# ConvFFN pairs of a decoder step: two weight sums and two low parts moved from VectorE to transfers that add

## The chip, the cores and the metric

The kernel runs on one core of one Trainium2 chip. The metric is the device time of one execution in microseconds; the median of three runs is given. The core has TensorE (PE; its weight loads are shown as PEld), VectorE (DVE), ScalarE (ACT), GpSimd (POOL) and SyncE (SP), and 16 DMA engines that all queues share.

## The reference

One layer of a hybrid decoder is computed for 512 prompt tokens and 8 x 8 sample tokens, 576 in all: a normalized input projection, a short convolution branch and a windowed attention branch, their merge, and then a ConvFFN. The change is in the ConvFFN, which is, cut to what matters:

```python
h2 = _rmsnorm(x, norm2_g) * (1.0 + sc2) + sh2
a, val = jnp.split(h2 @ w_up, 2, axis=-1)          # 1024 x 2 * 2816
ac, new_ffn = _causal_conv(a, ffn_buf, ffn_conv_w)   # width 3, along the tokens
x = x + g2 * ((jax.nn.gelu(ac, approximate=False) * val) @ w_down)
```

## The kernel before

All operands are float32. A product keeps that precision by a split: `hi` is the operand rounded to TensorE's fp32r (a copy by ScalarE), `lo` is source minus `hi` (a subtraction by VectorE), and a product is three matmuls, hi x hi, hi x lo and lo x hi. Weights are stationary tiles of 128 x 128; the tokens are the moving side.

The 2816 hidden columns are 22 tiles of 128, in groups 0 to 7, 8 to 15 and 16 to 21. After the hidden tiles of a group, the down-projection of that group adds to the residual: eight products, one for each 128 output columns. Tiles 0 to 3 are computed plainly. Tiles 4 to 21 are **pairs** (`FfnPair`): the gate tile and the value tile of the same number are computed together, as a product of 2 x 2 blocks by Winograd's scheme with seven block products instead of eight. The blocks are gate and value, the two halves of the inner dimension (4 slices of 128 each), and the two halves of the tokens (288 each).

Per pair, the weights are loaded as two tiles of 128 x 1024 (512 KB), `ra` for the value and `rb` for the gate, into the pool `raw` with four buffers. A DMA row is 512 B. With c0 and c1 for the first and second four slices, VectorE makes four sums of 128 x 512:

- `sums1` (lines 305 to 308): `s3 = ra.c0 + rb.c0`, and `rb.c0 += rb.c1`;
- `sums2` (lines 310 to 312): `ra.c0 += rb.c0`, and `ra.c1 += ra.c0`.

Four groups of weights are split in high and low parts: A is `ra` before its sums, B is `rb` after `sums1`, C is `ra` after `sums2`, D is `s3`. A, B and C are 128 x 1024 and go to pools `whi` and `wlo` with five buffers each; D is 128 x 512 and goes to slots of a common pool of 57. `pair_weights` gives these as steps with names: `ah` is the high part of A, `al` its low part, and so for `bh`, `bl`, `ch`, `cl`, `dh`, `dl`.

`pair_product` (lines 334 to 377) is the seven parts of 12 matmuls each; after part n it calls `steps[n]`. Part 1 uses A, part 2 C, part 3 B, part 4 A, part 5 B, part 6 D, part 7 C. The results of parts 1 and 3 are copied from their bank by ScalarE (`p`); VectorE forms the differences `uv`; and the gate and value are combined by VectorE, the last 64 tokens by POOL (lines 1536 and 1548).

While pair m runs, `beside_pair` (lines 1561 to 1571) prepares the weights of pair m+1 and does the rest of pair m-1 (convolution taps, gelu, product, split), and the loads of pair m+2 are issued. During a down-projection `in_turn` (lines 329 to 332) does the steps of the next group's first pair after the products 4 to 7. Ahead of pair 4 the steps are written out by hand between the products of tiles 2 and 3 (lines 1660 to 1683).

From the FFN on, TensorE, VectorE and ScalarE keep the program's order (`pinned`). The order on POOL and SyncE is set by a scheduler with a simulated timeline. Each engine and each queue works in the order that results. SyncE issues the loads; a load waits until its buffer is free. Lines 104 to 112 are a helper that issues the operations, so most instructions carry line 109; SyncE's weight loads carry line 148.

Of the kernel before, what the change touches and what calls it, by code (L numbers as in the profile page):

```python
# [10 lines left out]
F32 = mybir.dt.float32  # L11
F32R = mybir.dt.float32r
AF = mybir.ActivationFunctionType
ALU = mybir.AluOpType
AX = mybir.AxisListType

P = 128
D = 1024
NK = D // P
# [6 lines left out]
FF = 2816  # L26
# [9 lines left out]
S_BUFS = 5  # L36
# [33 lines left out]
def step_kernel(ctx: ExitStack, tc: tile.TileContext, ins: dict, outs: list):  # L70
    nc = tc.nc
# [5 lines left out]
    wp = ctx.enter_context(tc.tile_pool(name="wp", bufs=3))  # L77
# [8 lines left out]
    def nm(s):  # L86
        cnt[0] += 1
        return f"{s}{cnt[0]}"

    def slot(s, dt=F32, shape=None):  # L90
        return ap_.tile(shape or [P, NT], dt, tag="a", name=nm(s))
# [22 lines left out]
    pe, act, dve, pool = (InOrder(e) for e in (nc.tensor, nc.scalar, nc.vector, nc.gpsimd))  # L114
# [30 lines left out]
    def load_w(src, nk):  # L145

        raw = wp.tile([P, nk, P], F32, tag="raw", name=nm("raw"), bufs=W_BUFS)
        nc.sync.dma_start(raw, src)
        return raw
# [56 lines left out]
    def product(w, xs):  # L206
        ps = mmps()
        for k in range(len(xs)):
            kstep(halves(ps), w, xs, k)
            tick()  # L210
        return pf(ps)
# [17 lines left out]
    class PairOperands:  # L229
# [38 lines left out]
        def low(self):  # L268
            for lo, src, hi in ((self.tl, self.t, self.th), (self.nl, self.r[0][:, :HT], self.nh)):
                dve.tensor_tensor(out=lo, in0=src, in1=hi.bitcast(F32), op=ALU.subtract)  # L270
# [12 lines left out]
    def pair_weights(ra, rb):  # L283

        c0, c1 = slice(0, 4), slice(4, 8)
        w = {}

        def add(out, x, y):
            dve.tensor_tensor(out=out, in0=x, in1=y, op=ALU.add)

        def tiles():
            return [wp.tile([P, NK, P], F32R, tag=t, name=nm(t), bufs=S_BUFS) for t in ("whi", "wlo")]

        def high(name, src, get):
            w[name] = hi, lo = get()
            act.activation(hi, src, AF.Copy)

        def low(name, src):
            hi, lo = w[name]
            dve.tensor_tensor(out=lo, in0=src, in1=hi.bitcast(F32), op=ALU.subtract)  # L300

        def s3_slots():
            return slot("wh", F32R, [P, 4, P]), slot("wl", F32R, [P, 4, P])

        def sums1():
            w["raw"] = slot("s3", shape=[P, 4, P])
            add(w["raw"], ra[:, c0], rb[:, c0])
            add(rb[:, c0], rb[:, c0], rb[:, c1])

        def sums2():  # L310
            add(ra[:, c0], ra[:, c0], rb[:, c0])
            add(ra[:, c1], ra[:, c1], ra[:, c0])

        def named(n0, n1, name):
            hi, lo = w[name]
            w[n0] = (lambda k: hi[:, k, :]), (lambda k: lo[:, k, :])
            if n1:
                w[n1] = (lambda k: hi[:, k + 4, :]), (lambda k: lo[:, k + 4, :])

        def one(name, src, get, n0, n1):  # L320
            return (lambda: (high(name, src(), get), named(n0, n1, name))), (lambda: low(name, src()))

        ah, al = one("A", lambda: ra, tiles, "a0", "a1")
        dh, dl = one("D", lambda: w["raw"], s3_slots, "s3", None)
        bh, bl = one("B", lambda: rb, tiles, "s1", "b1")
        ch, cl = one("C", lambda: ra, tiles, "s2", "s4")
        return w, dict(sums1=sums1, sums2=sums2, ah=ah, al=al, bh=bh, bl=bl, ch=ch, cl=cl, dh=dh, dl=dl)

    def in_turn(t):

        order = {0: "sums1 ah al", 2: "dh dl sums2", 3: "bh bl", 4: "ch cl"}
        return {at: (lambda names=names: [t[n]() for n in names.split()]) for at, names in order.items()}
# [46 lines left out]
    def kpm(w, m0, k0=0, nk=NK):  # L379
        return w[k0 * P : (k0 + nk) * P, m0 : m0 + P].rearrange("(k p) m -> p k m", p=P)  # L380
# [311 lines left out]
    for x in range(2):  # L692
        for y in range(2):
            c = slice(2 * y, 2 * y + 2)
            tc.keep_in_program_order(nc.gpsimd.dma_start(xT_dram[x, :, c], xTt[x][:, c]))
    kT = []
    for j in (2, 0, 1):
        t = slot("kT")
# [20 lines left out]
    for raw in raws:  # L719
        hi = wp.tile([P, 4, 256], F32R, tag="whi", name=nm("whi"), bufs=S_BUFS)  # L720
        lo = wp.tile([P, 4, 256], F32R, tag="wlo", name=nm("wlo"), bufs=S_BUFS)
# [14 lines left out]
    for i in range(5):  # L736
        ps = aux()
        for k in range(NK):
            whi, wlo = (x[:, k % 4, :] for x in wv[k // 4])
# [9 lines left out]
    for i in (3, 4):  # L749
# [3 lines left out]
        t = slot("kout", shape=[P, 256])  # L753
# [21 lines left out]
    def queries(t, ps=None):  # L775
# [52 lines left out]
        out=sel,  # L828
        in0=snk.rearrange("p (h g) -> p h g", h=4),
        in1=ind.unsqueeze(1).to_broadcast([P, 4, 4]),  # L830
        op=ALU.mult,
# [331 lines left out]
    for m in range(NK):  # L1163
        if m in (5, 6):
            src, dst = ((ins["cache_k_win"], nks), (ins["cache_v_win"], nvs))[m - 5]
# [15 lines left out]
        if m == 1:  # L1181
# [9 lines left out]
            out=b10(u)[:, :, 2:10], in0=b8(sv(ps)), in1=b8(sv(c_sb)), op=ALU.mult  # L1191
# [44 lines left out]
    for m in range(NK - 1):  # L1236
        w = weights(kpm(wco, m * P), NK)
# [6 lines left out]
    w, steps = pair_weights(*raws[0])  # L1244
# [55 lines left out]
    def residual(ps, xt, blk, c0=0, c1=NT):  # L1300

        p1 = min(c1, 512)
        dve.scalar_tensor_tensor(
            out=xt[:, c0:p1], in0=ps[:, : p1 - c0], scalar=modT[:, blk, 0:1], in1=xt[:, c0:p1],
            op0=ALU.mult, op1=ALU.add,
        )
        if c1 > 512:
            t = sp.tile([P, 64], F32, tag="rt", name=nm("rt"))
            dve.tensor_tensor(
                out=b8(t), in0=b8(ps[:, p1 - c0 :]), in1=bc(modT[:, blk, 1:9]), op=ALU.mult  # L1310
            )
            dve.tensor_tensor(out=sv(xt), in0=sv(xt), in1=t, op=ALU.add)
# [196 lines left out]
    class FfnPair(FfnTile):  # L1509


        def __init__(self, m):
            super().__init__(m)
            self.raws = [load_w(kpm(w_up, c + m * P), NK) for c in (FF, 0)]

        def prepare(self):
            self.w, self.steps = pair_weights(*self.raws)
            return self.steps

        def run(self, steps):  # L1520
# [40 lines left out]
    def beside_pair(p, t):  # L1561

        none = lambda: None
        f = lambda n: t[n] if t else none
        g = lambda n: getattr(p, n) if p else none
        return {
            0: [f("ah"), g("first_tap"), f("sums1"), f("al"), g("taps")],
            1: [f("dh"), f("bh"), g("gelu")],
            2: [f("dl"), f("sums2"), f("bl"), g("times")],
            4: [f("ch"), g("high"), f("cl"), g("low")],  # L1570
        }

    def down_load(m, m0, m1):
# [87 lines left out]
    nxt = FfnPair(5)  # L1661
    ops[3].sums()
    ops[3].high()
    steps["ah"]()
    a3 = product(w_a3, h2)
    value(tiles[2], v2)
    tiles[2].low()
    ops[3].low()
    steps["sums1"]()
    steps["al"]()  # L1670
    steps["dh"]()
    steps["bh"]()
    steps["dl"]()
    v3 = product(w_v3, h2)
    start(tiles[3], a3)
    steps["sums2"]()
    tiles[3].taps()
    tiles[3].gelu()
    steps["ch"]()
    steps["bl"]()  # L1680
    steps["cl"]()
    value(tiles[3], v3)
    tiles[3].low()

# [2 lines left out]
    for m0, m1 in FCH:  # L1687
# [3 lines left out]
        for m in range(max(m0, 4), m1):  # L1691
            pair = pairs.pop(m)
            beside = [{0: n3}] if m == 4 else []
            if m + 1 < m1:
                if m + 2 < m1:
                    pairs[m + 2] = FfnPair(m + 2)
                beside.append(beside_pair(before, pairs[m + 1].prepare()))
            else:
                wd = {}
                raw = [down_load(j, m0, m1) for j in range(2)]  # L1700
                beside.append(beside_pair(before, None))
                beside.append({2: [lambda: wd.update({0: split_w(raw[0])})],
                               4: [lambda: wd.update({1: split_w(raw[1])})]})
            pair.run(merged(*beside))
            before = pair
# [6 lines left out]
        if m1 < NF:  # L1712
            pairs = {m1: FfnPair(m1)}
            steps = None
            ps = [mmps() for _ in range(2)]
            n = m1 - m0
            for k0, k1 in ((0, n - 2), (n - 2, n)):
                for j in range(2):
                    for k in range(k0, k1):
                        kstep(halves(ps[j]), wd[j], fa, k)  # L1720
            wd[2] = split_w(down_load(2, m0, m1))
            for j in range(2):
                residual(pf(ps[j]), x1[j], 40 + j)
            for m in range(2, NK):
                if m + 1 < NK:
                    wd[m + 1] = split_w(down_load(m + 1, m0, m1))
                acc_m = product(wd[m], fa)
                if m == 4:
                    steps = in_turn(pairs[m1].prepare())
                    steps[0]()  # L1730
                elif m > 4:
                    steps[m - 3]()
                if m == NK - 1:
                    pairs[m1 + 1] = FfnPair(m1 + 1)
                residual(acc_m, x1[m], 40 + m)
            continue
        pinned.clear()
# [105 lines left out]
```

## Time and profile before

| what | value |
|---|---|
| median of three runs | 1001.3 us (1000.7 to 1001.51) |
| span of the profiled execution | 999.2 us; no other time is given for it |
| busy, PE / PEld / DVE / ACT / POOL | 983.2 / 942.1 / 672.2 / 449.6 / 100.4 us |
| granted TensorE clock | 0.998 |
| DMA | 119.18 MB, mean 119 GB/s |

Pair 4 starts at about 640 us, the last pair ends at about 946 us. Busy time of an engine doesn't say that it bounds: what counts is which wait ends last. A busy TensorE isn't TensorE at its peak, as the ends of matmuls are modelled. Names in the rows are those of the program without numbers, so the tile `s3` is shown as `s`, and all `raw` tiles as `raw`.

### The profile page before, as it was taken

How to read it: one execution, taken by the hardware profiler on the slowest of the kernel's cores; microseconds unless marked ns; L12 is line 12 of the kernel's file. 1: busy time of each engine (PE TensorE's matmuls, PEld its weight loads, DVE VectorE, ACT ScalarE, POOL GpSimd, SP SyncE). 2: the span in 40 equal slices, each digit the busy share in tenths (PEclk: the TensorE clock that was granted, in tenths of full speed). 3: DMA queues.
4: the chain of work that ended last, by engine and by line, in shares of the span. 5: the costliest groups of instructions: out<-in, count | busy, mean ns of one | idle time of the engine just before them, and what ended most of it. 6: DMA issues, size and time to landing. Idle time of an engine off the chain costs nothing.

```text
span 999.2 us, 18724 instructions
## 1 busy us (share of the span) xinstructions
PE 983.2 (98%) x7516; PEld 942.1 (94%) x7516; DVE 672.2 (67%) x1243; ACT 449.6 (45%) x837; POOL 100.4 (10%) x271
## 2 busy tenths in 40 slices
PE   7999999999999999999999999999999999999997
PEld 6799999999989889999889999999999999999997
DVE  5637666666563367888454568896569995579954
ACT  5354545444544225545232347554225553235453
POOL 2222111100010000000000021011001110001120
PEclk9999999999999999999999999999999999999999
DMA  9983322333423822235972302233233222323302
GB/s 305 320 247 95 107 84 78 93 110 111 141 65 88 289 97 85 86 103 156 342 230 73 107 6 79 65 85 106 85 95 95 86 85 86 106 67 100 110 9 95
DMA packets 173481, 119.18 MB, mean 119 GB/s; under 512 B 6887, under 2 KB 160846, under 8 KB 173106
## 3 DMA queue, kind: packets, MB, share of 16 engines
q1 hardware_dynamic: 169954, 107.00, 35.1%
q0 software_dynamic: 3296, 10.73, 3.4%
q8 instruction: 59, 0.97, 0.4%
q14 instruction: 28, 0.23, 0.1%
q10 hardware_dynamic: 144, 0.26, 0.1%
HBM read 109.17 MB, written 7.35 MB: 117 GB/s over the span
## 4 chain that ended last, share of the span: by engine, by line
PE 88%; DVE 5%; ACT 2%; DMA 2%; issue 2%; SPq 0%; POOL 0%; POOLq 0%; DVEq 0%; ACTq 0%
PE mm L109 64%; PE aux L109 21%; PE aux L1104 2%; PE aux L1019 1%; DMA ad<-in_w_ada 1%; DVE wlo L109 1%; DMA raw<-in_w_in 1%; ACT whi L109 1%; SPq L385 0%; DVE raw L109 0%; DVE cy L109 0%; ACT y L109 0%; DVE uv L109 0%; DVE tl L109 0%; DVE fl L109 0%
## 5 line engine op out<-in xcount | busy, mean ns | idle before, releaser
L109 ACT ACTIVATE whi<-raw 128x1024 fp32r<-128x1024 f32 (+3 forms) x166 | 168.1, 1024 | 200.8 <-PE mm L109 106.9
L109 DVE TENSOR_TENSOR wlo<-raw,whi 128x1024 fp32r<-128x1024 f32 (+3 forms) x166 | 195.3, 1183 | 48.3 <-ACT whi L109 46.2
L109 PE MATMUL mm<-hh,whi 128*128 128x256 f32 (+2 forms) x560 | 127.6, 304 | 0.5 <-ACT hh L109 0.5
L109 PE MATMUL mm<-hh,wlo 128*128 128x256 f32 (+2 forms) x560 | 122.1, 295 | 0.0
L109 PE MATMUL mm<-hl,whi 128*128 128x256 f32 (+2 forms) x560 | 121.0, 295 | 0.1
L109 PEld LDWEIGHTS mm<-hh,whi 128*128 128x128 f32 x560 | 91.6, 188 | 8.1 <-issue 6.6
L109 PEld LDWEIGHTS mm<-hl,whi 128*128 128x128 f32 x560 | 93.7, 188 | 0.7 <-DVE hl L109 0.5
L109 PEld LDWEIGHTS mm<-hh,wlo 128*128 128x128 f32 x560 | 94.2, 188 | 0.0
L109 DVE SCALAR_TENSOR_TENSOR x<-mm,modT,x 128x512 f32<-128x512 f32 (+1 forms) x33 | 22.6, 686 | 70.6 <-PE mm L109 70.5
L109 PE MATMUL mm<-fl,whi 128*128 128x256 f32 (+1 forms) x304 | 65.4, 296 | 0.0
L109 PE MATMUL mm<-fh,whi 128*128 128x256 f32 (+1 forms) x304 | 64.8, 295 | 0.3 <-DVE rt L109 0.3
L109 PE MATMUL mm<-fh,wlo 128*128 128x256 f32 (+1 forms) x304 | 64.7, 294 | 0.0
L109 PE MATMUL mm<-th,whi 128*128 128x288 f32 x208 | 61.6, 296 | 0.7 <-DVE uv L109 0.7
L109 PE MATMUL mm<-th,wlo 128*128 128x288 f32 x208 | 61.4, 295 | 0.5 <-DVE wlo L109 0.5
L109 PE MATMUL mm<-tl,whi 128*128 128x288 f32 x208 | 61.2, 294 | 0.0
L109 PEld LDWEIGHTS mm<-fh,whi 128*128 128x128 f32 x304 | 50.6, 188 | 0.5 <-PE mm L109 0.5
L109 PEld LDWEIGHTS mm<-fh,wlo 128*128 128x128 f32 x304 | 51.0, 188 | 0.0
L109 PEld LDWEIGHTS mm<-fl,whi 128*128 128x128 f32 x304 | 50.9, 188 | 0.0
L109 PE MATMUL aux<-2h,whi 128*128 128x288 f32 (+2 forms) x160 | 47.3, 295 | 0.8 <-ACT p L109 0.8
L109 PE MATMUL aux<-2h,wlo 128*128 128x288 f32 (+2 forms) x160 | 47.2, 295 | 0.0
L109 PE MATMUL aux<-2l,whi 128*128 128x288 f32 (+2 forms) x160 | 47.0, 294 | 0.0
L870 ACT ACTIVATE s<-s,nmx 128x256 f32<-128x256 f32 (+1 forms) x72 | 34.1, 475 | 25.5 <-DVE nmx L867 17.4
(310 smaller groups left out, 2569.8 us busy)
## 6 DMA issues: line engine op xcount, KB each, us to landing
raw<-in_w_in SPq DMA_DIRECT2D x52, 512.0 KB, 4.2
raw<-in_w_up SPq DMA_DIRECT2D x44, 512.0 KB, 3.8
ada<-in_w_ada SPq DMA_DIRECT2D x64, 256.0 KB, 6.0
ad<-in_w_ada SPq DMA_DIRECT2D x32, 256.0 KB, 6.3
raw<-in_w_down SPq DMA_DIRECT2D x16, 512.0 KB, 3.5
raw<-in_w_conv_out SPq DMA_DIRECT2D x8, 512.0 KB, 3.5
raw<-in_w_attn_out SPq DMA_DIRECT2D x8, 512.0 KB, 3.5
raw<-in_w_mix_out SPq DMA_DIRECT2D x8, 512.0 KB, 5.6
```

The lines of the kernel that those rows point to most:

```text
L109: done = getattr(self.engine, name)(*args, **kwargs)
L870: nc.scalar.activation(s[x // 2][:, x % 2, :w], s[x // 2][:, x % 2, :w], AF.Exp, bias=nmx[:, x : x + 1], accum_out=den[:, x : x + 1],)
L1019: done = nc.tensor.matmul(O[HALF[par], :256], vt(i - nkt + 1 + kt)[:, hd * 64 : hd * 64 + 64], pts[kt][:, par * 256 : par * 256 + 256], st ...
L1104: done = nc.tensor.matmul(ps[32 * j : 32 * j + 32, :], cT[:, k, :], cols[k][j], start=(k == 1), stop=(k == NK - 2),)
```

## The change

1. The pair allocates `s3` itself, and SyncE loads `ra.c0` a second time into it (256 KB, from the value columns). `sums1` becomes two transfers issued by POOL that read DRAM and add to what is in SBUF: the first four slices of the gate columns onto `s3`, the second four onto `rb.c0`. VectorE's two sums go.
2. The low parts of B and C: ScalarE writes the high part, then a second copy with scale -1 writes `lo = -hi`, and a transfer issued by POOL from SBUF to SBUF adds the source, so that `lo = source - hi`. VectorE's two subtractions go. A and D are split as before.
3. The steps move: beside a pair, `sums2` and B come after part 1, D after part 2, C after part 3, and the `sums1` of pair m+2 are asked for after part 4. In a down-projection, `sums1` come after product 3, A and `sums2` after product 4, B after 5, D and C after 6, and the second pair of the next group is loaded and summed after product 7. Ahead of pair 4 the order by hand is changed in the same sense.

The number of matmuls doesn't change.

```diff
+    def add_transfer(out, src):
+        return pool.dma_start(out, src, accum_op=ALU.add)
+
+    def pair_weights_moved(ra, rb, s3):
...
+        def ah():
+            w["A"] = hi, lo = tiles()
+            act.activation(hi, ra, AF.Copy)
+            named("a0", "a1", "A")
+        def low(name, src):
+            hi, lo = w[name]
+            dve.tensor_tensor(out=lo, in0=src, in1=hi.bitcast(F32), op=ALU.subtract)
+        def sums2():
+            dve.tensor_tensor(out=ra[:, c0], in0=ra[:, c0], in1=rb[:, c0], op=ALU.add)
+            dve.tensor_tensor(out=ra[:, c1], in0=ra[:, c1], in1=ra[:, c0], op=ALU.add)
...
+        def moved(name, src, n0, n1):
+            w[name] = hi, lo = tiles()
+            act.activation(hi, src, AF.Copy)
+            act.activation(lo, hi.bitcast(F32), AF.Copy, scale=-1.0)
+            named(n0, n1, name)
+            add_transfer(lo.bitcast(F32), src)
...
+    def in_turn_moved(t):
+        order = {0: "ah al sums2", 2: "b", 3: "dh dl c"}
...
 class FfnPair(FfnTile):
             self.raws = [load_w(kpm(w_up, c + m * P), NK) for c in (FF, 0)]
+            self.s3 = slot("s3", shape=[P, 4, P])
+            nc.sync.dma_start(self.s3, kpm(w_up, FF + m * P, 0, 4))
+
+        def sums1(self):
+            m = self.m
+            add_transfer(self.s3, kpm(w_up, m * P, 0, 4))
+            add_transfer(self.raws[1][:, 0:4], kpm(w_up, m * P, 4, 4))
...
 beside_pair
-            0: [f("ah"), g("first_tap"), f("sums1"), f("al"), g("taps")],
-            1: [f("dh"), f("bh"), g("gelu")],
-            2: [f("dl"), f("sums2"), f("bl"), g("times")],
-            4: [f("ch"), g("high"), f("cl"), g("low")],
+            0: [f("ah"), g("first_tap"), f("al"), g("taps")],
+            1: [f("sums2"), f("b"), g("gelu")],
+            2: [f("dh"), f("dl"), g("times")],
+            3: [f("c")],
+            4: [g("high"), g("low")],
...
 ahead of pair 4
     ops[3].high()
+    pair.sums1()
     steps["ah"]()
     a3 = product(w_a3, h2)
     value(tiles[2], v2)
     tiles[2].low()
     ops[3].low()
-    steps["sums1"]()
     steps["al"]()
+    steps["sums2"]()
+    steps["b"]()
+    v3 = product(w_v3, h2)
     steps["dh"]()
-    steps["bh"]()
     steps["dl"]()
-    v3 = product(w_v3, h2)
+    steps["c"]()
+    nxt.sums1()
     start(tiles[3], a3)
-    steps["sums2"]()
     tiles[3].taps()
     tiles[3].gelu()
-    steps["ch"]()
-    steps["bl"]()
-    steps["cl"]()
     value(tiles[3], v3)
...
 beside a pair, and in a down-projection
+                if m + 2 < m1:
+                    beside.append({4: [pairs[m + 2].sums1]})
...
-                    steps = in_turn(pairs[m1].prepare())
+                    steps = in_turn_moved(pairs[m1].prepare())
...
+                if m == 3:
+                    pairs[m1].sums1()
                 if m == NK - 1:
                     pairs[m1 + 1] = FfnPair(m1 + 1)
+                    pairs[m1 + 1].sums1()
```

More of the change, by code (lines that the diff above doesn't have):

```diff
@@ L327, in pair_weights, with tiles, named, dh @@
         return w, dict(sums1=sums1, sums2=sums2, ah=ah, al=al, bh=bh, bl=bl, ch=ch, cl=cl, dh=dh, dl=dl)
+    def add_transfer(out, src):
+        return pool.dma_start(out, src, accum_op=ALU.add)
+    def pair_weights_moved(ra, rb, s3):
+        w = {}
+        c0, c1 = slice(0, 4), slice(4, 8)
+        def tiles():
+            return [wp.tile([P, NK, P], F32R, tag=t, name=nm(t), bufs=S_BUFS) for t in ("whi", "wlo")]
+        def named(n0, n1, name):
+            hi, lo = w[name]
+            w[n0] = (lambda k: hi[:, k, :]), (lambda k: lo[:, k, :])
+            if n1:
+                w[n1] = (lambda k: hi[:, k + 4, :]), (lambda k: lo[:, k + 4, :])
+        def ah():
[3 more added lines that the diff above has]
+        def low(name, src):
+            hi, lo = w[name]
+            dve.tensor_tensor(out=lo, in0=src, in1=hi.bitcast(F32), op=ALU.subtract)
+        def sums2():
+            dve.tensor_tensor(out=ra[:, c0], in0=ra[:, c0], in1=rb[:, c0], op=ALU.add)
+            dve.tensor_tensor(out=ra[:, c1], in0=ra[:, c1], in1=ra[:, c0], op=ALU.add)
+        def dh():
+            w["D"] = hi, lo = slot("wh", F32R, [P, 4, P]), slot("wl", F32R, [P, 4, P])
+            act.activation(hi, s3, AF.Copy)
+            named("s3", None, "D")
+        def moved(name, src, n0, n1):
[4 more added lines that the diff above has]
+            add_transfer(lo.bitcast(F32), src)
+        return w, dict(
+            sums2=sums2, ah=ah, al=lambda: low("A", ra), dh=dh, dl=lambda: low("D", s3),
+            b=lambda: moved("B", rb, "s1", "b1"), c=lambda: moved("C", ra, "s2", "s4"),
+        )
+    def in_turn_moved(t):
+        order = {0: "ah al sums2", 2: "b", 3: "dh dl c"}
+        return {at: (lambda names=names: [t[n]() for n in names.split()]) for at, names in order.items()}
     def in_turn(t):
@@ L1514, in __init__ @@
             self.raws = [load_w(kpm(w_up, c + m * P), NK) for c in (FF, 0)]
+            self.s3 = slot("s3", shape=[P, 4, P])
[4 more added lines that the diff above has]
+            add_transfer(self.raws[1][:, 0:4], kpm(w_up, m * P, 4, 4))
         def prepare(self):
-            self.w, self.steps = pair_weights(*self.raws)
+            self.w, self.steps = pair_weights_moved(*self.raws, self.s3)
             return self.steps
@@ L1728, in step_kernel @@
                 if m == 4:
-                    steps = in_turn(pairs[m1].prepare())
+                    steps = in_turn_moved(pairs[m1].prepare())
                     steps[0]()
-                elif m > 4:
+                elif m > 4 and m - 3 in steps:
                     steps[m - 3]()
+                if m == 3:
+                    pairs[m1].sums1()
                 if m == NK - 1:
                     pairs[m1 + 1] = FfnPair(m1 + 1)
+                    pairs[m1 + 1].sums1()
                 residual(acc_m, x1[m], 40 + m)
```

## The prediction

> **What bounds the kernel now.** I read the page's busy times first, then the waits of TensorE from 480 us on, then the chain of waits and a table of stretches in the pair stage, and last the DMA views.
>
> ```profile
> PE 983.2 (98%) x7516; PEld 942.1 (94%) x7516; DVE 672.2 (67%) x1243; ACT 449.6 (45%) x837; POOL 100.4 (10%) x271
> ```
> ```profile
> PE aux L109 <- ACT p L109: 0.8, 1, 0.8
> PE mm L109 <- DVE uv L109: 0.7, 3, 0.3
> PE mm L109 <- DVE wlo L109: 0.5, 1, 0.5
> PE mm L109 <- DVE rt L109: 0.3, 1, 0.3
> PE mm L109 <- ACT sq L109: 0.2, 1, 0.2
> ```
> TensorE is busy for 98% of the span, and after 480 us it waits 2.5 us in all. The first three of these waits, 2.0 us, belong to the pairs that the change touches. So the change can win little; how much it can lose is the question.
>
> One part of a pair product is 12 matmuls (chain of waits), seven parts are a pair, and the stretches give a pair's period (columns: us, busy us of PE, PEld, DVE, ACT and POOL with counts, clock, DMA share, GB/s):
>
> ```profile
> 748.78 1.58 PE aux L109 x12
> ```
> ```profile
> 739.26:750.37 11.11, 11.11 (x87) 11.11 (x86) 9.37 (x15) 5.31 (x7) 0.82 (x3) 1.00 0.34 94
> 772.58:783.67 11.09, 11.09 (x87) 11.09 (x86) 10.95 (x17) 6.04 (x9) 1.40 (x5) 1.00 0.31 92
> 806.40:818.02 11.62, 11.36 (x84) 11.16 (x85) 11.48 (x19) 5.41 (x8) 1.76 (x6) 1.00 0.31 93
> ```
> Bound by TensorE, a pair takes 11.11 us (7 x 1.58). Where VectorE has piled up work (11.48 us busy of 11.62) the pair takes 0.51 us longer. The DMA engines are a third busy.
>
> **The change, part by part.** *Engines.* The rows of the affected operations:
>
> ```profile
> L109 ACT ACTIVATE whi<-raw x15: 1040/1049/1065, 640.3 to 698.3; 128x1024 fp32r<-128x1024 f32 x15
> L109 DVE TENSOR_TENSOR wlo<-raw,whi x14: 1215/1218/1226, 639.6 to 692.6; 128x1024 fp32r<-128x1024 f32 x14
> L109 DVE TENSOR_TENSOR raw<-raw x6: 691/692/693, 646.9 to 672.4; 128x512 f32<-128x512 f32 x6
> L109 DVE TENSOR_TENSOR s<-raw,raw x3: 680/681/684, 646.2 to 666.5; 128x512 f32<-128x512 f32 x3
> ```
> VectorE loses per pair two low parts and two sums: 2 x 1.22 + 0.69 + 0.68 = 3.8 us, so about 11.5 becomes 7.7 us. ScalarE gains two negated copies, 2 x 1.05 = 2.1 us: the 6.0 us of the second stretch become 8.1. Both then lie under the 11.11 us of TensorE. The three waits for `uv` (0.51 us each by the periods) and the one for `p` (0.8 us) go: **-2.3 us**. The `wlo` wait gets a new cause, below.
>
> *The new path.* A low part of B or C was ready one VectorE instruction after its high part. Now it needs a negation on ScalarE, an issue on POOL and a transfer of 512 KB that adds. No DMA of the trace adds, so I call its time from issue to landing T and bound it by transfers of the same queue:
>
> ```profile
> xT_dram<-xT POOLq DMA_DIRECT2D x4, 576.0 KB, 6.4
> x<-xT_dram POOLq DMA_DIRECT2D x2, 1152.0 KB, 8.5
> q<-low POOLq DMA_DIRECT2D x16, 128.0 KB, 3.2
> ```
> Lower end 3.2 us: the 128 KB between two SBUF tiles. Upper end 8.5 us: an add reads source and destination, 1024 KB, nearest to the 1152 KB row. I take the row nearest in size, 576 KB: **T = 6.4 us**, and keep 3.2 and 8.5 for the range. [...]
>
> *The loop on POOL.* In the changed program's order POOL does, in the run of pair m: the transfer of B(m+1), the add into `raw` of pair m+2, the product `cy` of pair m-1, the transfer of C(m+1), the gate sum of pair m. It is in order, so C(m+1) stands behind an add that waits for the load of pair m+2. With four `raw` buffers, SyncE's load of pair m+2 waits until the transfer C(m) has read its source. So C(m) and C(m+1) are linked: C(m) lands, SyncE loads 512 + 256 + 512 KB, POOL issues the add, does `cy`, issues C(m+1).
>
> ```profile
> DMA to landing us min/median/max: 3.5/4.3/4.9
> ```
> ```profile
> GB/s 0 164 219 264 63 0 0 0 13 265 252 169 0 11 0 30 268 167 217 23 0 0 0 68 288 216 138 0 0 44 303 180 172 0 0 0 69 279 12 0
> ```
> ```profile
> L791 POOL DMA_DIRECT2D q<-low x16 | 8.4, 524 | 47.7 <-DVE low L787 20.3 <-PE aux L109 12.4 <-DVE den L877 7.3
> L1548 POOL TENSOR_TENSOR cy<-uv,y 128x64 f32<-128x64 f32 x18 | 5.8, 325 | 80.1 <-ACT y L109 80.1
> ```
> A lone load of 512 KB in the window 640 to 700 lands in 3.5 us; 768 KB (786 thousand bytes) behind it at the 303 GB/s of the best slice add 2.6: 6.1 us. One issue is 0.52 us, `cy` 0.33. The loop is 6.1 + 0.52 + 0.33 + T = 6.95 + T = 13.35 us against 11.11. TensorE needs C's low part at the third matmul of part 2, so each link makes a run 2.24 us longer. Links: C(4) to C(6) two, C(9) to C(14) five, C(17) to C(20) three (the last pair of a group has no load ahead of it). Ten by 2.24: **+22.4 us**.
>
> *The direct path* of a C outside the loop (C(7), C(9), C(15), C(17), C(21); step 3 follows part 3, for the first of a group I use the same figure as bound):
>
> ```profile
> 671.35 0.38 ACT L109 COPY p<-mm 128x288 f32<-128x288 f32 x1
> ```
> From the first use (third matmul of part 2) to the end of part 3 is 2 x 1.58 - 0.26 = 2.9 us (two matmuls of 0.13); the bank's copy 0.38, high part and negation 2.1, then T: 11.8 us, 0.7 too long. Five of them: **+3.4 us**.
>
> *Into pair 4.* Here VectorE is the late engine now:
>
> ```profile
> 633.19 0.45 DVE L109 TENSOR_TENSOR nl<-t,nh 128x288 fp32r<-128x288 f32 x1
> 642.65 0.40 PE L109 MATMUL mm<-th,wlo 128*128 128x288 f32 x1 [0.54 <-DVE wlo L109]
> 646.66 0.40 PE L109 MATMUL aux<-2h,whi 128*128 128x288 f32 x1 [0.84 <-ACT p L109]
> ```
> After `nl` (633.6) come A's low part 1.2, the two sums 1.4, then ScalarE 2.1: 638.3, and with T 644.7 instead of 642.65: **+2.1 us**. At T under 4.3 this is no loss, and under 3.6 the 0.54 us is won.
>
> *What costs nothing.* The `s3` load and its add (256 KB each) and B's transfer lie beside C's: B is issued two parts earlier and is due one part later. SyncE's extra issues delay only loads, counted in the 6.1. In the down-projections the steps lie in products of 48 matmuls, 6.4 us each, with a product or more to spare. If that cover fails there, it costs up to T once per group. POOL's gate sum now stands behind C's issue, 0.5 us; ScalarE's first tap of the next run waits for it, and has 3 us of slack (8.1 of 11.1 us busy).
>
> Sum: -2.3 + 22.4 + 3.4 + 2.1 = +25.6. The profiled execution spans 999.2 us, 2.1 under the median of the runs, 1001.3; I keep that distance. **1001.3 + 25.6 = 1026.9 us, 2.6% slower.**
>
> **The rivals.** *Hidden (the other side: faster).* If T is at most 4.16 us, the loop fits into 11.11 us and no transfer is late. Then the waits for `uv` (1.5), `p` (0.8) and, below 3.6, `wlo` (0.5) go: 998.5 us, 0.3% faster. For it: 128 KB took 3.2 us, DMA is a third busy. Against it: 576 KB took 6.4, and loads and adds now overlap. T between 4.16 and about 4.5 gives no change.
>
> *The DMA engines themselves become the bound.*
>
> ```profile
> q1 hardware_dynamic: 169954, 107.00, 35.1%
> q0 software_dynamic: 3296, 10.73, 3.4%
> ```
> The first queue moved 107.00 MB in 35.1% of 999.2 us of all engines, 305 GB/s; the second 10.73 MB in 3.4%, 316 GB/s. A full run now has 1.31 MB of plain loads (4.3 us) and adds of 1.57 MB; if an add occupies the engines for both reads, 3.15 MB, 10.0 us. Together 14.3 us, 3.2 over. Twelve runs (4, 5, 8 to 13, 16 to 19) carry all of it: 38, with 3.4 + 2.1 - 2.3: 1042 us. With one read it is 9.3 us and hidden. [...]
>
> *Slow adds.* T = 8.5: the loop is 15.45 us, 10 x 4.34; direct path 5 x 2.8; pair 4 +4.2; less 2.3: 1001.3 + 59.3 = 1061 us.
>
> *The loop is not closed* (buffers come free earlier than I read it): then only the direct path counts, 15 x 0.7 + 2.1 - 2.3: 1012 us.
>
> **How the numbers follow.** Forecast 0.45, DMA engines 0.16, slow adds 0.13, open loop 0.08, hidden 0.18, of which 0.10 faster and 0.08 no change (0.2%, 2 us, is about what a measurement of this kernel can tell from none). Slower: 0.45 + 0.16 + 0.13 + 0.08 = 0.82. The range goes from 1000 (within the hidden case) to 1062 (T = 8.5), leaving out 0.10 below and some 0.06 above.
>
> **What would show it.** Right: TensorE waits about 2 us per run in part 2 for the DMA of `wlo`, periods of 13 to 14 us in runs 10 to 13, POOL idle before the add into `raw`, `wlo` landing in 5 to 8 us; VectorE near 7.7 us per pair. Wrong: `wlo` landing under 4.2 us or periods of 11.1; or DMA share near 1 in those runs, which is the second rival; or TensorE waiting for ScalarE or VectorE, which I have excluded.

## The result, and the profile after

The changed kernel takes 1062.5 us (median of four runs, 1053.2 to 1067.6) against 1001.0 us before: ratio 1.0603 with a 95% interval of 1.0553 to 1.0654, 6% slower. The forecast had the sign (slower, 1026.9 us) and less than half of the size: +61.5 us instead of +25.6, and just past the range's upper end of 1062. The profiled execution took 1064.4 us and spans 1062.6, 63.4 more than before.

I read the same views in the same order as for the kernel before. First the busy times of the page, then TensorE's waits from 480 us on (us in total, times, longest; 0.2 us for `sq` stand there as before):

```profile
PE 1002.2 (94%) x7516; PEld 958.1 (90%) x7516; DVE 610.6 (57%) x1171; ACT 486.6 (46%) x873; POOL 176.8 (17%) x343
```
```profile
PE mm L109 <- DMA wlo<-raw: 45.7, 16, 8.1
PE mm L109 <- DVE uv L109: 0.8, 1, 0.8
```
Two things are to be seen. TensorE now waits 46.7 us where it waited 2.5, nearly all of it for the transfer that adds into `wlo`. And the same 7516 matmuls are busy for 1002.2 us instead of 983.2, at a mean granted clock of 0.977 instead of 0.998. 44.2 + 19.0 = 63.2 us: that is the whole difference. The four runs differ in the same way, 1053.2 us at a clock of 0.988 and 1067.6 at 0.977.

The stretches from one first use of C's low part to the next, in the middle of a group; the first and the last of four (columns as in the prediction):

```profile
784.80:800.70 15.90, 12.69 (x84) 12.45 (x84) 8.20 (x15) 8.96 (x13) 4.36 (x8) 0.91 0.84 174
...
833.40:850.27 16.87, 13.86 (x84) 13.62 (x84) 8.10 (x14) 8.05 (x11) 6.46 (x12) 0.80 0.80 158
```
These four pairs take 15.9 to 16.9 us; I had said 13 to 14. The 84 matmuls themselves take 12.7 to 13.9 us instead of 11.1. VectorE and ScalarE are far from full, at 8.1 to 8.2 and 8.0 to 9.0 us. The DMA share times the stretch, 0.84 x 15.90 and 0.80 x 16.87, is 13.4 and 13.5 us of busy DMA engines per pair; the two stretches between have 14.4 and 14.2.

The chain of waits shows what makes up one such period (start us, us, what; one turn of it, and the first pieces of two later ones):

```profile
784.82 4.49 PE mm L109 x22
789.31 1.47 PE aux L109 x11
...
790.81 1.07 ACT whi L109
...
791.90 1.07 ACT wlo L109
792.97 0.35 issue
793.31 7.34 DMA wlo<-raw
...
800.70 4.72 PE mm L109 x22
...
833.38 5.65 PE mm L109 x22
```
The 22 `mm` matmuls are the last ten of part 2 and part 3; the 11 `aux` matmuls are part 4. So the high part of the next pair's C does not start after part 3 but after part 4. Then come high part, negation and the transfer, and TensorE has to wait for it at the third matmul of the next part 2. No step of the chain is on POOL or SyncE except the issue of 0.35 us.

The matmuls right behind such a wait (timeline of TensorE; in brackets the idle time before):

```profile
784.82 0.61 PE L109 MATMUL mm<-th,wlo 128*128 128x288 f32 x1 [4.48 <-DMA wlo<-raw]
785.22 0.44 PE L109 MATMUL mm<-th,whi 128*128 128x288 f32 x1
...
787.95 0.29 PE L109 MATMUL mm<-th,whi 128*128 128x288 f32 x1
788.08 0.29 PE L109 MATMUL mm<-tl,whi 128*128 128x288 f32 x1
```
They start 0.24 us apart, and after some 2.8 us again 0.13 us apart. Eight such slow stretches together add some 16 us, most of the 19 us by which the matmuls got longer.

Last, POOL's queue and the issues of the transfers into `wlo` (queue: packets, MB, share of the 16 engines; issue: count, KB each, median us to landing):

```profile
q0 software_dynamic: 27488, 39.04, 19.6%
...
wlo<-raw POOLq DMA_DIRECT2D x36, 512.0 KB, 6.9
```
POOL's queue moved 28.3 MB more than before and took 16 points more of all engines. The transfers that add land in 6.9 us; my T was 6.4. So the length of the transfer was forecast nearly right, and the time around it was not.

### The profile page after: what moved, and what is told of

Read it like the earlier page. It is cut to its first block, busy times and chain, and to the rows that moved or that the text cites. A ratio compares the mean times of both kernels' runs of the same rounds, so it can differ in the third digit from the quotient of the medians.

```text
span 1062.6 us, 18947 instructions
## 1 busy us (share of the span) xinstructions
PE 1002.2 (94%) x7516; PEld 958.1 (90%) x7516; DVE 610.6 (57%) x1171; ACT 486.6 (46%) x873; POOL 176.8 (17%) x343
## 4 chain that ended last, share of the span: by engine, by line
PE 77%; DMA 13%; ACT 4%; issue 3%; DVE 1%; POOL 1%; SPq 0%; POOLq 0%; DVEq 0%; ACTq 0%
PE mm L109 59%; PE aux L109 16%; DMA wlo<-raw 7%; DMA raw<-in_w_up 3%; PE aux L1158 1%; ACT whi L109 1%; PE aux L1073 1%; DMA ad<-in_w_ada 1%; ACT wlo L109 1%; DMA raw<-in_w_in 1%; SPq L439 0%; ACT y L109 0%; DVE y L109 0%; DVE wlo L109 0%; DVE ol L109 0%
## 5 line engine op out<-in xcount | busy, mean ns | idle before, releaser
L109 DVE TENSOR_TENSOR wlo<-raw,whi 128x1024 fp32r<-128x1024 f32 (+3 forms) x130 | 151.5, 1173 | 47.0 <-ACT whi L109 44.7
L109 PE MATMUL mm<-th,wlo 128*128 128x288 f32 x208 | 70.5, 339 | 45.7 <-DMA wlo<-raw 45.7
L109 PEld LDWEIGHTS mm<-th,wlo 128*128 128x128 f32 x208 | 45.7, 220 | 49.4 <-DMA wlo<-raw 49.4
L109 PE MATMUL mm<-th,whi 128*128 128x288 f32 x208 | 67.8, 326 | 0.1
L109 PE MATMUL mm<-tl,whi 128*128 128x288 f32 x208 | 67.6, 325 | 0.0
L109 POOL DMA_DIRECT2D wlo<-raw x36 | 38.3, 1081 | 132.9 <-ACT wlo L109 131.8
L109 DVE TENSOR_TENSOR fl<-cy,fh 128x576 fp32r<-128x576 f32 x22 | 16.7, 760 | 73.6 <-ACT fh L109 73.6
L109 DVE TENSOR_TENSOR uv<-mm,p 128x288 f32<-128x288 f32 x52 | 23.6, 454 | 49.4 <-PE mm L109 49.1
```

Source lines behind the costliest of these rows:

```text
L109: done = getattr(self.engine, name)(*args, **kwargs)
```

## The experiments

Three theories of the period stood against one another: the direct path of C's low part (A), the loop on POOL that the prediction put first (B), and the DMA engines that the adds occupy. Beside them stood the question what the lower clock costs by itself. All runs are compared with the kernel before on the same chip (1001.2 to 1001.5 us).

**The sums alone.** The low parts of B and C are made by VectorE as before; the sums stay with the transfers.

```diff
-            act.activation(lo, hi.bitcast(F32), AF.Copy, scale=-1.0)
-            named(n0, n1, name)
-            add_transfer(lo.bitcast(F32), src)
+            named(n0, n1, name)
+            low(name, src)
```


> Part 1 of the change alone: the two sums by adding loads stay, the low parts of B and C are made by VectorE again. Theory A (the low part of C arrives late by its own path: end of part 4, high part, negation, transfer; each pause of TensorE is followed by some 3 us of matmuls at 0.24 instead of 0.13 us): no wait of TensorE for a transfer is left, 998 to 1003 us. Theory B (the loop on POOL: C behind the add of pair m+2, whose load waits for C): no C on POOL, so also 998 to 1003. Theory C (the DMA engines are the bound): adds fall from 1.5 to 0.5 MB per pair, 998 to 1005. The run tells what the first half costs by itself, not the theories apart.

Measured: 999.7 us, ratio 0.9983 (0.9973 to 0.9992). One stretch of a pair beside another:

```profile
772.50:783.60 11.10, 11.10 (x86) 11.10 (x85) 10.37 (x17) 6.47 (x9) 4.15 (x8) 1.00 0.80 167
```
TensorE never waits in this stretch, and the clock is full. The transfers that add two sums are harmless by themselves. The gain of 1.8 us fits the relief of VectorE, which the prediction put at 2.3 us for all four moves: TensorE waits 1.3 us after 480 us, where it had waited 2.5.

**The low parts alone.** VectorE makes the two sums, ahead of A's low part; `s3` is not loaded.

```diff
+        def sums1():
+            dve.tensor_tensor(out=s3, in0=ra[:, c0], in1=rb[:, c0], op=ALU.add)
+            dve.tensor_tensor(out=rb[:, c0], in0=rb[:, c0], in1=rb[:, c1], op=ALU.add)
...
-            nc.sync.dma_start(self.s3, kpm(w_up, FF + m * P, 0, 4))
```


> Part 2 of the change alone: the low parts of B and C by transfers as in the change, the two sums by VectorE again, no second load of the value columns. Theory A: C's own path is unchanged, only its transfer is less disturbed (6 instead of 7.4 us), so pairs still take 13 to 14 us: 1030 to 1045 us, with TensorE waiting for the transfer of C's low part in about 15 pairs and at a lowered clock. Theory B: no add stands ahead of C on POOL, the loop is open: 1000 to 1012 us. Theory C: per pair 1.05 MB of loads and 1.05 MB of adds, 3.4 + 6.6 = 10 us of the engines: below 11.1, so 998 to 1003 us.

Measured: 1033.0 us, 1.0304 (1.0276 to 1.0333). The waits of TensorE, then its chain of waits:

```profile
PE mm L109 <- DMA wlo<-raw: 24.2, 16, 3.0
```
```profile
761.15 3.17 PE mm L109 x22
764.32 1.47 PE aux L109 x11
...
768.42 5.12 DMA wlo<-raw
...
773.58 3.17 PE mm L109 x22
...
780.69 7.00 DMA wlo<-raw
...
787.73 4.69 PE mm L109 x22
```
There is no add of a sum in POOL's queue, so there is no loop, and yet half of the loss is there. It has the same chain over part 4. Theory A was right here, and what I had forecast for a path outside the loop, 0.7 us per pair, was wrong. With a transfer of 5.1 us the period is 12.4; after one of 7.0 us the matmuls come at the slow pace as well (4.69 instead of 3.17 us for 22).

**C's low part on VectorE.** B keeps the transfer, the sums too.

```diff
-            act.activation(lo, hi.bitcast(F32), AF.Copy, scale=-1.0)
             named(n0, n1, name)
-            add_transfer(lo.bitcast(F32), src)
+            if name == "C":
+                low(name, src)
+            else:
+                act.activation(lo, hi.bitcast(F32), AF.Copy, scale=-1.0)
+                add_transfer(lo.bitcast(F32), src)
```


> The change with the low part of C made by VectorE; the sums by adding loads and the low part of B by a transfer stay. Theory A: B is begun after part 1 and is due in part 3 of the next run, its path fits: 998 to 1005 us, clock back at about 0.998. Theory B: the loop goes on with B in C's place (B lands, the gate columns are loaded, added to, and B of the next pair stands behind that add): period about 14 us, 1025 to 1040 us. Theory C: adds 1.0 MB and loads 1.25 MB per pair, 4.3 + 6.6 = 10.9 us: just hidden, 998 to 1010 us.

Measured: 1027.4 us, 1.0252 (1.0233 to 1.0270). The two longest of the waits of TensorE in sum, and the timeline of POOL:

```profile
PE mm L109 <- DVE uv L109: 12.7, 7, 2.8
PE mm L109 <- DMA wlo<-raw: 6.1, 5, 3.3
```
```profile
774.21 1.29 POOL L109 DMA_DIRECT2D raw<-in_w_up  x1 [1.03 <-DMA raw<-in_w_up]
774.99 1.42 POOL L109 DMA_DIRECT2D wlo<-raw  x1
775.57 1.20 POOL L1612 TENSOR_TENSOR cy<-uv,y 128x64 f32<-128x64 f32 x1
...
788.92 1.31 POOL L109 DMA_DIRECT2D raw<-in_w_up  x1 [0.83 <-DMA raw<-in_w_up]
```
Theory B's number. A queue that works in order does make a loop: the add waits for its load, and B's transfer and the product `cy` stand behind it. One turn is 788.92 - 774.21 = 14.7 us. It acts for the most part through `cy`, by way of the split of the gelu product and VectorE's `uv` (12.7 us of waits), and for the smaller part through B's low part itself (6.1 us).

**Copies instead of adds.** This kernel leaves out what the adds compute: the two sums and the low parts of B and C.

```diff
-        return pool.dma_start(out, src, accum_op=ALU.add)
+        return pool.dma_start(out, src)
```


> The change with every adding transfer made a plain copy of the same tiles (the sums and the low parts of B and C come out as copies, so that part of the computation is left out). Same order, same waits. Theory A: the transfer of C gets shorter by what the second read costs; with 5 instead of 7.4 us a pair takes about 12 us: 1008 to 1022 us. Theory C: the engines have half the reads of the adds, 9.3 us per pair: 998 to 1003 us. If an add costs no more than a copy: 1055 to 1065 us, as the change itself.

Measured: 1017.4 us, 1.0154 (1.0135 to 1.0173). Landing of the transfers into `wlo`, waits of TensorE, and a stretch of one pair:

```profile
DMA to landing us min/median/max: 2.8/4.2/6.7
```
```profile
PE mm L109 <- DMA wlo<-raw: 13.8, 11, 2.5
```
```profile
753.23:764.34 11.11, 11.11 (x84) 11.11 (x84) 7.53 (x15) 7.86 (x10) 3.51 (x8) 1.00 0.72 236
```
The adding by itself costs 45 of the 61 us. The transfers land in 4.2 instead of 6.9 us, and the engines are busy for 0.72 x 11.11 = 8.0 us in this pair and for 8.9 and 9.0 in the two after it, instead of 13.4 to 14.4. The other 16 us are there without any add.

**Six buffers for high and low parts**, so that C need not wait for the buffer of A; three slots of the common pool are given up for it.

```diff
-A_BUFS = 57
+A_BUFS = 54
-S_BUFS = 5
+S_BUFS = 6
```


> The change with six instead of five buffers for the high and the low parts of weights (and 54 instead of 57 common slots, to make room). Theory A: the high part of C no longer waits until part 4 has released the high part of A, its path is 1.5 us shorter in some 15 pairs, pauses get shorter and the clock recovers in part: 1030 to 1048 us. Theory B (the loop on POOL sets the period): nothing on that loop changes, 1055 to 1065 us.

Measured: 1050.2 us, 1.0490 (1.0472 to 1.0508). The chain of waits:

```profile
760.19 6.99 DMA wlo<-raw
...
767.24 1.79 DMA raw<-in_w_up
...
771.68 0.07 POOL raw L109
...
772.49 0.76 POOL cy L1609
773.25 7.26 DMA wlo<-raw
...
785.59 1.07 ACT whi L109
...
788.10 8.14 DMA wlo<-raw
```
The high part now starts behind part 3 (785.59), which shows that the buffer of A had held it behind part 4. Only 12 us are won. In the first turn shown, the loop of the forecast is there link by link: C lands, SyncE loads, POOL adds, `cy`, the next C, from 760.19 to 773.25, 13.06 us, where the prediction had 13.35. But C's negation was done just then, too, 0.36 us before its transfer went out.

In the four turns after it, the transfer again goes out 0.4 to 0.5 us behind the negation, so the direct path still sets the period. It has become shorter by part 4 and longer by its transfer, which now lands in 8.1 to 9.1 us, where it took 7.1 to 7.7 in the change. In these turns the DMA engines are busy for 0.91 to 1.00 of the time; one of them:

```profile
796.28:811.50 15.22, 11.41 (x84) 11.19 (x84) 8.08 (x14) 8.32 (x12) 6.35 (x10) 1.00 1.00 193
```
That points to the DMA engines as what stands behind the path; no run tried it by itself. The expectation of A was missed by 2 us, B's by 5.

**C on VectorE, and POOL in program order** (B's transfer and `cy` ahead of the add for pair m+2); the edit of C is that of the third experiment.

```diff
-            pinned.extend([dve, act])
+            pinned.extend([dve, act, pool])
```


> The change with the low part of C on VectorE, as in an earlier run (1027 us), and with POOL's transfers kept in the order in which they are written: B of pair m+1, then the product of pair m-1, then the two adds of pair m+2. If the period of 14.7 us of that earlier run was the loop over POOL (B and the product behind the add that waits for a load, theory B's mechanism): it opens, 997 to 1001 us. If it was the amount of data: still 1020 to 1028 us.

Measured: 1006.0 us, 1.0055 (1.0038 to 1.0071). A stretch of 104 matmuls:

```profile
755.66:769.12 13.46, 13.46 (x104) 13.46 (x103) 10.26 (x18) 8.56 (x12) 6.49 (x11) 1.00 0.94 191
```
Taking `cy` and B from behind the add wins 21 of the 26 us: the loop in the kernel with C on VectorE was a matter of the order on POOL. What remains, 5 us over my expectation, is not settled; TensorE is busy in all of this stretch although the DMA engines are 94% busy, and the chain runs over the adds into `raw`.

**The change, and POOL in program order.** The same edit of `pinned`, with both low parts by transfer.

> The change with POOL's transfers kept in the order in which they are written: B, the product, C, and then the two adds of pair m+2; nothing else differs. Theory A (C's own path sets the period): little change, 1045 to 1062 us, TensorE waits for C's low part in about 15 pairs. Theory B (C behind the add sets it): the loop is open, 1000 to 1020 us.

Measured: 1082.6 us, 1.0815 (1.0796 to 1.0834), slower than the change itself. Neither theory held. The chain of waits:

```profile
784.17 11.14 DMA raw<-in_w_up
...
795.34 1.07 ACT whi L109
...
801.29 0.58 POOL wlo L109
...
802.64 10.40 DMA raw<-in_w_up
```
With the adds last, the add into `raw` goes out behind C's transfer and lands after 10 to 11 us; B of the next pair needs it, and C stands behind B. That is a third loop, of 802.64 - 784.17 = 18.5 us. The order on POOL that the scheduler had found was the better one here.

**Extra matmuls against the pauses.** At the head of part 2 of every pair product TensorE does 24 more matmuls into the same bank; the first real one overwrites them.

```diff
+            if at == 2:
+                for _ in range(24):
+                    matmul(bank, w["a0"][0](0), x["x00"][0][0], start=True, stop=True)
```


> The change with 24 more matmuls (3.2 us at full clock) at the head of part 2 of every pair, whose result is overwritten: 18 x 3.2 = 57 us of added matmul work, put where TensorE waits. If the slow matmuls after a pause are the clock's answer to the pause (theory A): the pauses that remain are short, matmuls stay at 0.13 us, pairs fall from 16 to about 14.4 us, the granted clock returns to 0.99 or more; less the added work in the pairs without a pause, 1042 to 1058 us: faster than the change although it does more. If the slow matmuls have another cause (transfers that load SBUF while TensorE reads it): they stay at 0.24 us, 1062 to 1085 us.

Measured: 1091.5 us, 1.0900 (1.0876 to 1.0924), outside what I had expected, because I had miscounted: 624 matmuls came in, not 432, since eight pair products stand ahead of the ConvFFN. The clock was 0.995 and TensorE busy for 1068.0 us; without 624 x 0.133 = 83 us that is 985, the 983 of the kernel before. The slow matmuls were gone but for one stretch, but 83 us are too much to compare times, so I did it again.

**The same in 15 of the 18 ConvFFN pairs only** (not in 4, 8 and 16).

```diff
+            if at == 2 and fill_part[0]:
...
+            fill_part[0] = self.m not in (4, 8, 16)
```


> As the run with 24 added matmuls, but only in the 15 ConvFFN pairs whose low part of C comes late (not in pairs 4, 8 and 16, nor in the pair products before the ConvFFN): 15 x 3.2 = 48 us of added work, overwritten. Theory A, with the pause as the cause of the slow matmuls: busy time of TensorE is 983 + 48 = 1031 and not 1002 + 48 = 1050, the granted clock is at 0.99 or more, and the time is that of the change or below, 1050 to 1062 us. If the slow matmuls have another cause: 1075 us or more, busy time near 1050.

Measured: 1061.8 us, 1.0598 (1.0583 to 1.0612). Busy times of the page and the waits of TensorE:

```profile
PE 1032.2 (98%) x7876; PEld 990.8 (94%) x7876; DVE 611.4 (58%) x1171; ACT 487.2 (46%) x873; POOL 177.8 (17%) x343
```
```profile
PE mm L109 <- DMA wlo<-raw: 9.2, 6, 4.7
```
360 matmuls more, 48 us of work, and the time is that of the change. 1032.2 - 48 = 984 us is the full pace, at a granted clock of 0.997. So the 19 us are shown to come from the pauses: with the pauses filled, the matmuls run at full pace beside the same transfers, and all but 1 of the 19 us is gone.

**B's low part alone by transfer**; C's and the sums on VectorE (the two edits for that are shown above).

> Only B's low part by a transfer; C's low part and both sums on VectorE, no second load. Theory A: B has part 1 to part 3 of the next run, 14.4 us less 4.5 of its own work and the issue: a transfer of 4.5 to 5.5 us fits, no add waits for a load on POOL; VectorE falls from 11.5 to about 10.3 us per pair and no longer stretches pairs to 11.62: 997.5 to 1000.5 us, as the sums alone or a little better than before. If a transfer that adds costs TensorE something by itself: above 1003 us.

Measured: 1000.2 us, 0.9988 (0.9979 to 0.9996). B's transfer, 4.6 us, is hidden, as forecast.

**C's low part used last**: in part 2 the eight matmuls with the high part come first.

```diff
+            if at == 2:
+                for n in range(3):
+                    for k in range(4):
+                        xh, xl = xs[k]
+                        wt, xx = ((hi(k), xh), (hi(k), xl), (lo(k), xh))[n]
+                        matmul(bank, wt, xx, start=k + n == 0, stop=k + n == 5)
...
```


> The change with the 12 matmuls of part 2 in another order: first the eight that use C's high part, then the four that use its low part, so the low part is first used at the ninth matmul instead of the third, 0.8 us later. Theory A (C's own path sets the period): 0.8 us less in some 15 pairs, and shorter pauses: 1042 to 1052 us. Theory B (loop on POOL) and theory C (DMA engines): no change, 1056 to 1066 us.

Measured: 1056.6 us, 1.0558 (1.0526 to 1.0590): 6 us less than the change, where A wanted 10 to 20. The interval overlaps that of the change (1.0553 to 1.0654), so this is no clear gain, and the time lies in the range of B and C. Timelines of ScalarE and of POOL in one turn:

```profile
788.87 1.06 ACT L109 ACTIVATE wlo<-whi 128x1024 fp32r<-128x1024 f32 x1
```
```profile
789.89 1.31 POOL L109 DMA_DIRECT2D raw<-in_w_up  x1 [5.08 <-DMA raw<-in_w_up]
...
790.93 1.48 POOL L109 DMA_DIRECT2D wlo<-raw  x1
```
Here C's transfer does stand behind the add on POOL, which had waited for its load: it goes out 1.0 us after C's negation is done. This is pair 11, whose transfer had gone out 0.4 us after the negation in the change: POOL's loop takes back most of the 0.8 us. In the next three pairs the transfer goes out 0.4 to 0.5 us behind the negation and lands in 6.7 to 8.1 us. So neither A alone nor B alone accounts for this run.

**The low parts alone, with both remedies of the direct path**: sums on VectorE, six buffers, C's low part last (all three edits are shown above).

> Only the low parts of B and C by transfers (the earlier run of this took 1033 us, pairs 12.4 to 14.2), now with both reliefs of C's own path at once: six instead of five buffers, so the high part of C needn't wait for part 4 (1.5 us), and the low part first used at the ninth matmul of part 2 (0.8 us). Theory A, as the only limit here, since no add waits for a load on POOL and the DMA engines are busy 9.3 us per pair: the path falls from 13.3 on the average to 11.0 us, TensorE's own time, the pauses and the slow matmuls go: 999 to 1008 us. If the transfers cost more than this path (their data beside TensorE's reads, or POOL): still 1020 us or more.

Measured: 1010.2 us, 1.0081 (1.0063 to 1.0099). Waits of TensorE:

```profile
PE mm L109 <- DMA wlo<-raw: 8.0, 7, 2.5
```
Where no loop stands behind, shortening the direct path wins 23 of 32 us. That shows the path; A's figure was missed by 2 us.

## Why the prediction was right in its direction and wrong in its size

**The step that failed is the direct path.** The prediction put it at 11.8 us, 0.7 too long, for five pairs, and let the loop carry the rest. In the change it sets the period of nearly all pairs: in 14 of the 16 waits C's transfer goes out 0.3 to 0.5 us after ScalarE's negation is done. In the middle of a group it is 14.6 us long before a single matmul slows down: at full pace 3.17 + 1.47 us from the first use to the end of part 4, 2.18 for high part and negation, 0.35 for the issue, 7.34 to 7.67 for the transfer. Against the forecast's terms:

- "Step 3 follows part 3" is true of the program's order and not of the time: C's high part takes the buffer that A's leaves, and A is read until the end of part 4. That is 1.36 us. Six buffers move it behind part 3, as the experiment shows. The buffer count, five, stood in the code; I had followed it for `raw` and not for `whi`.
- The transfer on the path takes 7.1 to 7.7 us, T was 6.4: 1.0 us. Issue and small gaps: 0.45.
- **Slow matmuls had no term at all.** They add 1.3 to 2.5 us to a turn (4.49 to 5.65 us for 22 matmuls, against 3.17) and 19 us in all. In the trace of before TensorE's longest wait from 480 us on is 0.8 us, so it has no case of this there. In the change, matmuls start 0.24 instead of 0.13 us apart for 2.8 to 5.5 us behind eight of the pauses, of 2.2 to 8.1 us; behind seven others, of 0.9 to 3.1 us, they don't.

14.6 + 1.3 to 2.5 = 15.9 to 17.1 us is what the stretches show. Where the transfer lands in 5.1 or 5.4 us and no slow matmul follows, the same path gives pairs of 12.3 and 12.6 us (pairs 21 and 7).

**The loop on POOL exists, and has about the forecast's size, but it seldom decides.** The kernel with six buffers shows one turn of it at 13.06 us against 13.35 forecast, the one with C on VectorE another loop at 14.7. In the change it holds C's transfer back in two pairs only, 5 and 10, near the beginning of a group, by 1.9 and 1.8 us. The negation for pair 10 in the timeline of ScalarE, and two transfers into `wlo` in that of POOL:

```profile
774.38 1.06 ACT L109 ACTIVATE wlo<-whi 128x1024 fp32r<-128x1024 f32 x1
```
```profile
777.25 1.43 POOL L109 DMA_DIRECT2D wlo<-raw  x1
...
793.31 0.90 POOL L109 DMA_DIRECT2D wlo<-raw  x1 [0.57 <-ACT wlo L109]
```
The first goes out right behind an add that POOL had sat waiting for, as forecast; the second, one pair later, has only waited for ScalarE's negation. Loop and path do not add up as ten links and five paths: in each pair the later one counts alone. So the largest term of the forecast, +22.4 us for the loop, is hardly in the result, and the loss came from a path that the forecast had put at +3.4 us and from slow matmuls that it had left out. That the sign came out right is in part luck. Pair 5, for which the forecast had one link of 2.24 us, has the longest wait, 8.1 us; the chain has its transfer as

```profile
653.83 10.34 DMA wlo<-raw
```
It was issued behind an add into `raw`, two adds onto `s` and another transfer into `wlo`, and it lands as late as any of the 36 (maximum 10.3 us).

**The DMA engines** were a rival with 14.3 us per pair, if an add occupies them for two reads. They were busy for 13.4 to 14.4 us, and for 8.0 to 9.0 with copies, so as far as the busy time goes the condition held. The engines were 80 to 88% busy, so they were not the last limit, but a floor some 2 us under it: with the pauses filled, turns of 14.5 and 15.0 us have them at 0.98 and 0.95, and with six buffers one of 15.2 us at 1.00. Beside the adds of sums the transfers into `wlo` also take longer: they land in 5.1 us without them, in 6.9 with them (medians).

So three limits lie within 2 us of one another: the direct path (14.6 us), the loops on POOL (13.1 to 14.7) and the DMA engines (13.4 to 15.2). That fits one remedy alone giving 12 us, another none that is clear, and a third, which closes a longer loop, costing 20. The time came back to that of before only in the two kernels where C's low part is made by VectorE and POOL has either no adds of sums or no transfer of B behind them.

**What held.** T, at 6.4 against a median of 6.9, though in part by luck: it was read off a plain transfer of 576 KB, and the transfer in question lands in 4.2 us as a copy and in 5.1 as an add with no sums beside it. Into pair 4: +2.1 forecast, and one of the 16 waits, 2.2 us, is there. The relief of VectorE: the sums alone win 1.8 us, forecast was 2.3 for all. B hidden: shown by its own run. No wait for a low part inside the down-projections. VectorE per pair 8.1 us, forecast 7.7; ScalarE 8.0 to 9.0, forecast 8.1. The issues on POOL were costed too low, at 0.52 us each; the page's group for the change has

```profile
L109 POOL DMA_DIRECT2D wlo<-raw x36 | 38.3, 1081 | 132.9 <-ACT wlo L109 131.8
```
1.08 us of POOL for each, which costs nothing on the direct path beyond its 0.35 us, but lengthens the loops.

**What stays open:** why some pauses bring the slow pace and others of like length don't; whether the DMA engines lengthen C's transfer where its path was shortened; what the last 9 us of the low parts with both remedies, and the last 5 us of C on VectorE with POOL in order, are made of. These were read from traces and not tried.

The best version seen is the one with the sums alone, 0.9983 (0.9973 to 0.9992), faster than both kernels and at the edge of what can be told from no change. B's transfer alone is at 0.9988 (0.9979 to 0.9996).

## What to carry to other kernels

When a step moves from a compute engine to a transfer, follow its whole path from the last reader of its *destination* buffer to the first use, with each pool's buffer count, before looking at queues: the program's place of a step says when it may be issued, not when it can start. Work out every limit of a period separately and take the largest, since removing one of three close limits can win little (here 12 of 61 us with six buffers). And where a forecast has TensorE pause in each turn as long as here, by 2.2 to 8.1 us, give the slower matmuls behind the pauses a term of their own (here 16 us in eight stretches).

## What the runs showed of the hardware that I had not expected

- After pauses of 2.2 to 8.1 us TensorE ran at half its pace for 2.8 to 5.5 us (0.24 instead of 0.13 us per matmul of 288 columns) in eight of 15 cases (2.2, 3.0, 3.2, 3.3, 3.4, 3.5, 4.5 and 8.1 us); after the other seven (0.9, 1.1, 1.7, 2.2, 2.5, 2.7 and 3.1 us) it didn't. 48 us of extra matmuls in the pauses cost no time (1061.8 us against 1062.5).
- A transfer of 512 KB in SBUF that adds landed in 4.4 to 10.3 us, median 6.9; as a copy in 2.8 to 6.7, median 4.2. Per pair, 1.57 MB as adds instead of copies kept the DMA engines busy for 4 to 6 us more.
- Issuing it took POOL 1.08 us on average; issuing the same transfer as a copy took 0.56.
